# An opening stage of a mixer layer: squares and key weight behind the high parts, low parts on VectorE, projections by halves

## Chip, cores and metric

One NeuronCore of a Trainium2 chip runs the whole program. The metric is device time of one execution in microseconds, as the median of several runs. TensorE (PE) multiplies matrices, VectorE (DVE) and ScalarE (ACT) work elementwise, GpSimd (POOL) does elementwise work and issues some DMAs, SyncE (SP) issues most DMAs. Each engine runs its own instructions in order.

## The reference, cut to what matters

One layer of a diffusion backbone works on 1152 tokens of width 1024: 1024 noisy tokens and 128 prompt tokens. The opening is the modulated norm and the first projections:

```
def trunk_layer(x, mod, ...):
    shift1, scale1, gate1, shift2, scale2, gate2 = jnp.split(mod, 6, axis=-1)
    h = rmsnorm(x, norm1) * (1 + scale1) + shift1
    mix, new_gla, new_hgrn = hybrid_mixer(h, ...)
    ...
def hybrid_mixer(h, ...):
    q_a, k_a, v_a, g_a, lr_a, q_b, f_b, i_b, g_b = jnp.split(h @ w_in, offsets, axis=-1)
    ...
```

`mod` is `silu(c) @ w_ada + b_ada`. After the projections come two groups of gated linear scans (forward and backward), an output projection, and a convolutional feed-forward layer.

## The kernel before

**Precision.** A product of two float32 matrices is made of three faster ones: each operand is split into a high part (the value rounded to the format `fp32r`) and a low part (the rest), and the kernel adds high x high, high x low and low x high. ScalarE copies the high part (line 133 for a weight, line 505 for the activations `h1h`), and `split_lo` (line 69) subtracts it to leave the low part (`wl`, `h1l`) on VectorE or GpSimd.

**Tiles.** Tokens come in nine tiles of 128, `xt`, and three tiles make a group of 384 (`g`). The groups are worked in the order 2, 1, 0; the text calls them first, second and last. The width of 1024 is eight slices `kt` of 128.

**Opening, step by step.** The modulation is computed by matmuls at line 421 in two halves; `ada_first(i)` turns half `i` into scale and shift columns. `norm_x` normalises one token tile: `rstd_of` sums its squares on ScalarE (line 391, with a read of the accumulator), VectorE makes the mean (`st`, line 392), GpSimd the power -1/2 (line 393), and VectorE scales the tile (line 398). `modulate` then, for each slice `kt`: three transposes on TensorE (line 491) into one of four PSUM buffers, a multiply-add to `tt` on VectorE (line 500) or, for some slices, ScalarE (line 496), the high part on ScalarE (line 505) and the low part (line 69). For the first group, the low parts of the first four slices are on VectorE; all others take GpSimd for even slices and VectorE for odd ones. Low-rank columns are multiplied in two parts of four matmuls (line 550) and copied out (`lrs`, line 577).

**Projections.** `proj_d` (line 519) multiplies one weight of 128 columns with one group: 24 matmuls, for each slice high x high, high x low and low x high. `evac` (line 528) copies the sum out on ScalarE (`qj`, `kj`). `wq` and `wk` are the first two weights of the queue `seq`; every weight's low part in the opening is on GpSimd. The first group's key projection is emitted after the second group's `modulate`, and so on down.

**What sets the order.** Code order gives priorities, and a list scheduler with a timeline of its own places each instruction on its engine; `tc.issue_after(x)` forbids placing an instruction ahead of `x`. `prefetch_w` starts the load of the next weights and their split; while `slots["hold"]` is set, the split is put aside in `slots["held"]` and emitted later by whoever takes it out. Weights have two raw buffers (`raw`) and three of high and of low parts.

After the opening, the value projections (line 639) and the scan of the first groups run together: `o` at line 868 makes the gate logits, `fb`, `Q`, `k`, `m` and `S` are the scan's factors, keys and scores, and `lv` (line 964) its level products on TensorE.

## Time and profile before

| | us |
|---|---|
| median of 3 runs | 1519.8 (1519.39 to 1520.59) |
| the profiled execution, its own time | 1521.21 |
| its span in the profile | 1519.4 |
| TensorE busy in the span | 1465.9 (96%) |
| VectorE busy | 1148.0 (76%) |
| ScalarE busy | 780.5 (51%) |
| GpSimd busy | 709.1 (47%) |

A row of the profile in order of time gives the start, the duration, the engine, the line, the operation, what it writes and reads with its shape, and a count if several are merged; in brackets stands the idle time of the engine before it and what ended it. A row that merges several (x4) spans from the first start to the last end. A row that begins with a name and three numbers divided by slashes gives the shortest, middle and longest duration in ns. The chain in order of time gives start, length, engine and line.

### The profile page before, as it was taken

The numbers are of one execution on the slowest core, as the hardware profiler recorded it, in microseconds if no ns is written. First come the engines' busy times: TensorE is split into PE (matmuls) and PEld (weight loads), VectorE is DVE, ScalarE is ACT, GpSimd is POOL, SyncE is SP. The second block draws the span as 40 slices with busy tenths as digits, with TensorE's granted clock in tenths as the row PEclk, the third lists the DMA queues.
The fourth block names the chain that finished last, engine by engine and source line by source line (L and its number), as shares of the span: only waits on it lengthen the run. The fifth ranks groups of instructions, "written<-read, shape, count | busy, mean of one in ns | idle before, by whom it ended". The sixth has DMA issues, their size and how long they took to land.

```text
span 1519.4 us, 31109 instructions
## 1 busy us (share of the span) xinstructions
PE 1465.9 (96%) x12494; PEld 1246.8 (82%) x12494; DVE 1148.0 (76%) x1731; ACT 780.5 (51%) x1517; POOL 709.1 (47%) x538
## 2 busy tenths in 40 slices
PE   6999999999999999999989999999999999999997
PEld 2799989999898998777777888888888877888886
DVE  3666566664565767755699999999999999689475
ACT  3575667555454555613764454444444444466444
POOL 1602123234233241222238999999999995100001
PEclk9999999999999999999999999999999999999999
DMA  9311111335435464867642655544644567979762
GB/s 341 132 44 48 47 54 52 118 96 190 141 106 183 121 197 128 322 243 245 227 140 76 196 174 123 141 123 135 196 120 137 168 167 228 352 255 371 238 190 115
DMA packets 173802, 253.79 MB, mean 167 GB/s; under 512 B 11828, under 2 KB 113698, under 8 KB 171738
## 3 DMA queue, kind: packets, MB, share of 16 engines
q1 hardware_dynamic: 150455, 173.52, 35.6%
q0 software_dynamic: 22592, 77.60, 16.5%
q8 instruction: 98, 1.61, 0.4%
q10 hardware_dynamic: 611, 0.68, 0.1%
q14 instruction: 46, 0.38, 0.1%
HBM read 191.93 MB, written 82.90 MB: 181 GB/s over the span
## 4 chain that ended last, share of the span: by engine, by line
PE 81%; DMA 5%; DVE 5%; issue 3%; ACT 3%; POOL 2%; SPq 0%; POOLq 0%; ACTq 0%; DVEq 0%
PE u L1774 25%; PE mm L625 15%; PE xb L2246 8%; PE yb L2246 6%; PE mm L639 5%; PE x L2005 4%; PE mm L777 3%; PE lv L964 3%; PE yb L2298 2%; PE u L1544 2%; DVE acc L1939 2%; PE x L1032 2%; PE mm L519 1%; DMA raw<-in_w_in_dram 1%; PE ada L1201 1%
## 5 line engine op out<-in xcount | busy, mean ns | idle before, releaser
L1939 DVE SCALAR_TENSOR_TENSOR acc<-u,convc,acc 128x945 f32<-128x945 f32 (+2 forms) x352 | 426.7, 1217 | 7.3 <-ACT acc L1927 0.2
L69 POOL TENSOR_TENSOR wl<-raw,wh 128x1024 fp32r<-128x1024 f32 x42 | 103.3, 2473 | 248.5 <-ACT wh L133 193.4
L625 PE MATMUL mm<-h1h,wh 128*128 128x384 f32 x528 | 185.0, 350 | 0.8 <-ACT qj L528 0.8
L625 PE MATMUL mm<-h1l,wh 128*128 128x384 f32 x528 | 179.0, 339 | 0.0
L625 PE MATMUL mm<-h1h,wl 128*128 128x384 f32 x528 | 179.0, 339 | 0.0
L927 DVE TENSOR_TENSOR Q<-Q,fb 128x384 f32<-128x384 f32 x126 | 81.0, 643 | 82.2 <-PE lv L964 81.3
L69 POOL TENSOR_TENSOR wul<-sr,wuh 128x512 fp32r<-128x512 f32 (+1 forms) x64 | 123.9, 1935 | 14.4 <-ACT wuh L1759 14.3
L69 POOL TENSOR_TENSOR wul<-ra,wuh 128x1024 fp32r<-128x1024 f32 x44 | 117.6, 2673 | 19.1 <-ACT wuh L1759 19.1
L917 ACT ACTIVATE m<-k 128x384 f32<-128x384 f32 x126 | 70.2, 557 | 82.9 <-DVE k L929 40.8
L2220 POOL TENSOR_TENSOR sq<-sq,mhalf 128x1 f32<-128x1 f32 x9 | 11.1, 1232 | 205.3 <-DVE sq L2217 205.3
L625 PEld LDWEIGHTS mm<-h1h,wh 128*128 128x128 f32 x528 | 99.5, 188 | 5.7 <-issue 3.9
L625 PEld LDWEIGHTS mm<-h1l,wh 128*128 128x128 f32 x528 | 99.5, 188 | 0.6 <-issue 0.2
L625 PEld LDWEIGHTS mm<-h1h,wl 128*128 128x128 f32 x528 | 99.3, 188 | 0.8 <-issue 0.5
L929 DVE TENSOR_TENSOR k<-k,fb 128x384 f32<-128x384 f32 x126 | 76.5, 607 | 12.1 <-ACT m L917 7.3
L639 PE MATMUL mm<-wh,h1h 128*128 128x256 f32 x288 | 83.8, 291 | 1.1 <-ACT v L664 0.9
L639 PE MATMUL mm<-wh,h1l 128*128 128x256 f32 x288 | 80.5, 279 | 0.0
L639 PE MATMUL mm<-wl,h1h 128*128 128x256 f32 x288 | 80.4, 279 | 0.0
L133 ACT ACTIVATE wh<-raw 128x1024 fp32r<-128x1024 f32 x50 | 52.8, 1058 | 40.5 <-PE mm L625 11.2
L2037 POOL TENSOR_TENSOR acc<-acc,acc 128x1152 f32<-128x1152 f32 x22 | 62.3, 2834 | 14.8 <-DVE acc L1939 14.8
L1967 ACT ACTIVATE u2p<-u 128x512 f32<-128x512 f32 x44 | 26.4, 601 | 77.8 <-PE u L1774 77.8
L1759 ACT ACTIVATE wuh<-ra 128x1024 fp32r<-128x1024 f32 x42 | 44.3, 1054 | 34.6 <-issue 18.4
L1759 ACT ACTIVATE wuh<-sr 128x512 fp32r<-128x512 f32 (+1 forms) x62 | 48.0, 775 | 19.3 <-PE x L2005 14.4
(386 smaller groups left out, 4483.5 us busy)
## 6 DMA issues: line engine op xcount, KB each, us to landing
ra<-in_w_ffn_up_dram SPq DMA_DIRECT2D x84, 256.0 KB, 3.4
raw<-in_w_in_dram SPq DMA_DIRECT2D x32, 512.0 KB, 4.6
v<-in_w_ada_dram SPq DMA_DIRECT2D x27, 512.0 KB, 4.7
scr_g<-acc POOLq DMA_DIRECT2D x22, 576.0 KB, 5.5
scr_s<-late POOLq DMA_DIRECT2D x11, 1024.0 KB, 5.6
scr_t<-in_w_ffn_down_dram POOLq DMA_DIRECT2D x16, 704.0 KB, 7.3
wa<-in_w_ada_dram SPq DMA_DIRECT2D x16, 512.0 KB, 5.5
scr_t<-in_w_ffn_down_dram POOLq DMA_DIRECT2D x2, 2816.0 KB, 13.0
```

Of the source, the lines that this page charges most:

```text
L69: return eng.tensor_tensor(out, full, hi.bitcast(F32), op=ALU.subtract)
L625: anchor["fill"] = mm(ps, a[:, kt, :], h[kt][b], start=(n == 0), stop=(n == 23))
L639: anchor["fill"] = mm(ps, h[kt][t // 3][:, ts_], a[:, kt % 4, :], start=(n == 0), stop=(n == 23))
L917: nc.scalar.activation(aps(t, 0, [[2 * h, NB], [h, 2], [1, h]]), aps(src, 0, [[2 * h, NB], [BL + h, 2], [1, h]]), AF.Copy)
L927: nc.vector.tensor_tensor(qm, qm, aps(ff_, 2 * h - 1, [[BL - h, 2], [2 * h, NB], [0, h]]), op=ALU.mult)
L929: nc.vector.tensor_tensor(km, km, aps(ff_, BL + 2 * h - 1, [[-(BL + h), 2], [2 * h, NB], [0, h]]), op=ALU.mult)
L1759: first = nc.scalar.activation(hi, raw, AF.Copy)
L1774: last = mm(dst, w_slot(c, a, x)[:, kt, :], HB[y][b][:, kt, :], start=(start and n == 0), stop=(stop and n == 11), skip_group_check=True,)
L1939: last = nc.vector.scalar_tensor_tensor(o, u3[:, r0 + dy : r1 + dy, c0 + dx : c1 + dx], wc(3 * (dy + 1) + dx + 1), o, op0=ALU.mult, op1=AL ...
L2005: last = mm(pk, HB[h]["p"][:, 4 * half + kt, :], aps(flat(W[x]), a * 512 + kt * P, [[(b - a) * 512, 2], [1, P]]), start=(half + kt + n == ...
L2037: last = nc.gpsimd.tensor_tensor(accg, accg, accu, op=ALU.mult)
L2246: anchor["down"] = mm(banks[i], w[a][:, ts_], w[b][:, 512:1024], start=(start and j == 0 and n == 0), stop=(j == NPAIR - 1 and n == 2), sk ...
```

## The change

Six edits, all in the opening:

- The key weight's split is held back at its prefetch (`hold`) and emitted after the first group's `modulate`, to be placed after the first group's last high part (`anchor["first"] = anchor["hi"]`).
- The sums of squares of the other two groups are placed after the key weight's high part (`anchor["first"] = anchor["split"]`).
- The key weight's low part is on VectorE.
- All eight low parts of the first group are on VectorE.
- `proj_d` takes the slices in two halves of four, and in each half all high x high, then all high x low, then all low x high.
- The key projection of each group directly follows its query projection.

```
@@ -130,7 +130,7 @@
         else:
             anchor["load"] = nc.sync.dma_start(raw, srcs)
         def split():
-            nc.scalar.activation(hi, raw, AF.Copy)
+            anchor["split"] = nc.scalar.activation(hi, raw, AF.Copy)
             split_lo(eng, lo, raw, hi)
 
         if slots["hold"]:
@@ -179,8 +179,8 @@
 
 
     seq = []
-    def seq_cols(c):
-        seq.append((1, lambda: w_cols(w_in, c, nc.gpsimd)))
+    def seq_cols(c, eng=nc.gpsimd):
+        seq.append((1, lambda: w_cols(w_in, c, eng)))
 
     def seq_wide(c):
         seq.append((2, lambda: w_wide(w_in, [c], nc.gpsimd)))
@@ -195,7 +195,7 @@
 
     for tau in range(2):
         seq_cols(tau * P)
-        seq_cols(256 + tau * P)
+        seq_cols(256 + tau * P, nc.gpsimd if tau else nc.vector)
         seq_wide(512 + 256 * tau)
     for tau in range(2):
         for i in range(2):
@@ -388,7 +388,8 @@
         if junk is None:
             junk = sq_pool.tile([P, D], BF16, name="junk", tag="junk" + tag, bufs=1)
         st = sq_pool.tile([P, 2], F32, name="st", tag="st" + tag, bufs=4)
-        nc.scalar.activation(junk, x, AF.Square, accum_out=st[:, 0:1])
+        with after("first"):
+            nc.scalar.activation(junk, x, AF.Square, accum_out=st[:, 0:1])
         nc.vector.tensor_scalar(st[:, 0:1], st[:, 0:1], 1.0 / D, EPS, op0=ALU.mult, op1=ALU.add)
         anchor["pow"] = nc.gpsimd.tensor_tensor(st[:, 1:2], st[:, 0:1], mhalf[:, 0:1], op=ALU.pow)
         return st
@@ -440,7 +441,9 @@
     for t in (3, 4, 5, 0, 1, 2):
         load_x(t)
         if t == 5:
+            slots["hold"] = True
             prefetch_w(2)
+            slots["hold"] = False
 
     pt = ps_x.tile([P, 512], F32, name="x", tag="x")
     nc.tensor.transpose(pt[:, 0:P], vrow, ident)
@@ -502,7 +505,7 @@
                 )
             h_, l_ = hi(kt, g), lo(kt, g)
             for (c0, c1, hp_), (_, _, lp_) in zip(h_, l_):
-                nc.scalar.activation(hp_, t[:, c0:c1], AF.Copy)
+                anchor["hi"] = nc.scalar.activation(hp_, t[:, c0:c1], AF.Copy)
                 split_lo(lo_eng[kt % len(lo_eng)], lp_, t[:, c0:c1], hp_)
             if each is not None:
                 each(kt, t)
@@ -514,10 +517,11 @@
         hi, lo = w
         ps = ps_mm.tile([P, BL], F32, name="mm", tag="mm")
         n = 0
-        for kt in range(KT):
+        for kts in (range(4), range(4, KT)):
             for a, h in ((hi, h1h), (hi, h1l), (lo, h1h)):
-                mm(ps, a[:, kt, :], h[kt][b], start=(n == 0), stop=(n == 23))
-                n += 1
+                for kt in kts:
+                    mm(ps, a[:, kt, :], h[kt][b], start=(n == 0), stop=(n == 23))
+                    n += 1
         return ps
 
     def new_pj(nm):
@@ -568,7 +572,7 @@
                 lambda k, g: [(0, BL, h1l[k][g])],
                 ((ps_o, "o"), (ps_lv, "lv")),
                 tp,
-                (nc.vector,) if g == 2 and i == 0 else (nc.gpsimd, nc.vector),
+                (nc.vector,) if g == 2 else (nc.gpsimd, nc.vector),
                 lr_part,
                 (1, 3, 5) if g == 2 else (2, 5),
                 range(4 * i, 4 * i + 4),
@@ -577,16 +581,16 @@
         nc.scalar.activation(lrs, plr, AF.Copy)
         nc.scalar.dma_start(scr_lr[g], lrs)
         if g == 2:
+            anchor["first"] = anchor["hi"]
+            with after("first"):
+                slots["held"].pop(0)()
+            anchor["first"] = anchor["split"]
             wq = next_w()
             first_q[2] = evac(proj_d(wq, 2), "qj", 0.125)
             wk = next_w()
-        elif g == 1:
-            first_k[2] = evac(proj_d(wk, 2), "kj")
-            first_q[1] = evac(proj_d(wq, 1), "qj", 0.125)
         else:
-            first_k[1] = evac(proj_d(wk, 1), "kj")
-            first_q[0] = evac(proj_d(wq, 0), "qj", 0.125)
-            first_k[0] = evac(proj_d(wk, 0), "kj")
+            first_q[g] = evac(proj_d(wq, g), "qj", 0.125)
+        first_k[g] = evac(proj_d(wk, g), "kj")
     mraw = wap_.tile([P, 7, P], F32, name="mraw", tag="wa")
     nc.sync.dma_start(mraw, ins["masks"])
     nc.vector.tensor_copy(masks, mraw)
```

On ScalarE in the first group's second half, the order before was as follows (`h1h4` to `h1h7` are high parts of the first group, `junk` the squares of a token tile, `wh_326` the key weight's high part, `lrs` the low-rank copy):

```order
L391 ACTIVATE junk_544,st_545<-xt_319 128x1024
L505 ACTIVATE h1h4_378<-tt_466 128x384
L133 ACTIVATE wh_326<-raw_325 128x1024
L505 ACTIVATE h1h5_381<-tt_475 128x384
L577 ACTIVATE lrs_502<-mm_412 128x384
L391 ACTIVATE junk_550,st_551<-xt_321 128x1024
L505 ACTIVATE h1h6_384<-tt_484 128x384
L578 DMA scr_lr2_116<-lrs_502 128x384
L391 ACTIVATE junk_556,st_557<-xt_323 128x1024
L505 ACTIVATE h1h7_387<-tt_493 128x384
```

Now on ScalarE, from the same place:

```order
L508 ACTIVATE h1h4_376<-tt_464 128x384
L508 ACTIVATE h1h5_379<-tt_473 128x384
L508 ACTIVATE h1h6_382<-tt_482 128x384
L508 ACTIVATE h1h7_385<-tt_491 128x384
L133 ACTIVATE wh_326<-raw_325 128x1024
L392 ACTIVATE junk_571,st_572<-xt_319 128x1024
L581 ACTIVATE lrs_500<-mm_410 128x384
L392 ACTIVATE junk_577,st_578<-xt_321 128x1024
L582 DMA scr_lr2_116<-lrs_500 128x384
L532 ACTIVATE qj_530<-mm_505 128x384
L392 ACTIVATE junk_583,st_584<-xt_323 128x1024
```

The four high parts moved ahead of the squares and the key weight, and the copy of the query projection now stands ahead of the third square.

On VectorE at the passage from the first group to the second, the order before (`st` is a tile's mean of squares, `xt` its scaling, `masks` the cast of a constant, `tt` a multiply-add of the second group):

```order
L69 TENSOR_TENSOR h1l7_411<-tt_493,h1h7_387 128x384
L392 TENSOR_SCALAR st_693<-st_693 128x1
L398 TENSOR_SCALAR xt_323<-xt_323,st_557 128x1024
L398 TENSOR_SCALAR xt_331<-xt_331,st_693 128x1024
L392 TENSOR_SCALAR st_699<-st_699 128x1
L500 TENSOR_SCALAR tt_567<-x_563,s1_0_340,b1_0_342 128x384
L500 TENSOR_SCALAR tt_575<-x_571,s1_0_340,b1_0_342 128x384
L500 TENSOR_SCALAR tt_591<-x_587,s1_0_340,b1_0_342 128x384
L398 TENSOR_SCALAR xt_333<-xt_333,st_699 128x1024
L592 CAST masks_72<-mraw_867 128x896
```

Now on VectorE, from the scaling of token tile 5 (`xt_323`) on:

```order
L399 TENSOR_SCALAR xt_323<-xt_323,st_584 128x1024
L393 TENSOR_SCALAR st_720<-st_720 128x1
L393 TENSOR_SCALAR st_726<-st_726 128x1
L399 TENSOR_SCALAR xt_329<-xt_329,st_720 128x1024
L596 CAST masks_72<-mraw_867 128x896
L598 CAST low_masks_73<-mraw_867 32x160
L503 TENSOR_SCALAR tt_594<-x_590,s1_0_338,b1_0_340 128x384
L598 CAST low_masks_73<-mraw_867 32x160
L503 TENSOR_SCALAR tt_602<-x_598,s1_0_338,b1_0_340 128x384
L399 TENSOR_SCALAR xt_331<-xt_331,st_726 128x1024
L598 CAST low_masks_73<-mraw_867 32x160
L503 TENSOR_SCALAR tt_618<-x_614,s1_0_338,b1_0_340 128x384
```

The casts, a scaling and two means (tiles 0 and 1) moved ahead of the second group's multiply-adds, which now stand between casts.

On TensorE before the second group's query projection, the order before (`mm_638` is the first group's key projection, `x` a transpose, `mm_562` a low-rank part):

```order
L550 MATMUL mm_562<-tt_575,wlr_311 32x384
L550 MATMUL mm_562<-tt_567,wlr_311 32x384
L491 MATMUL x_623<-ident_74,xt_319 128x128
L491 MATMUL x_623<-ident_74,xt_321 128x128
L491 MATMUL x_623<-ident_74,xt_323 128x128
L519 MATMUL mm_638<-h1h0_366,wh_326 128x384
L519 MATMUL mm_638<-h1l0_390,wh_326 128x384
L519 MATMUL mm_638<-h1h0_366,wl_327 128x384
```

Now on TensorE, from the end of the first group's key projection (`mm_544`) to the second group's first transposes:

```order
L523 MATMUL mm_544<-h1l7_409,wh_326 128x384
L523 MATMUL mm_544<-h1h4_376,wl_327 128x384
L523 MATMUL mm_544<-h1h5_379,wl_327 128x384
L523 MATMUL mm_544<-h1h6_382,wl_327 128x384
L523 MATMUL mm_544<-h1h7_385,wl_327 128x384
L494 MATMUL x_590<-ident_74,xt_319 128x128
L494 MATMUL x_598<-ident_74,xt_319 128x128
L494 MATMUL x_606<-ident_74,xt_319 128x128
```

The whole key projection of the first group moved ahead of the second group's transposes, of which all 24 and a low-rank part now follow it in one piece. The same rows show the halves: the low weights come last.

More of the change, by code (lines that the diff above doesn't have):

```diff
@@ L132, in split @@
         def split():
-            nc.scalar.activation(hi, raw, AF.Copy)
+            anchor["split"] = nc.scalar.activation(hi, raw, AF.Copy)
             split_lo(eng, lo, raw, hi)
@@ L390, in rstd_of @@
         st = sq_pool.tile([P, 2], F32, name="st", tag="st" + tag, bufs=4)
-        nc.scalar.activation(junk, x, AF.Square, accum_out=st[:, 0:1])
+        with after("first"):
+            nc.scalar.activation(junk, x, AF.Square, accum_out=st[:, 0:1])
         nc.vector.tensor_scalar(st[:, 0:1], st[:, 0:1], 1.0 / D, EPS, op0=ALU.mult, op1=ALU.add)
@@ L442 @@
         if t == 5:
+            slots["hold"] = True
             prefetch_w(2)
+            slots["hold"] = False
     pt = ps_x.tile([P, 512], F32, name="x", tag="x")
@@ L516, in proj_d @@
         n = 0
-        for kt in range(KT):
+        for kts in (range(4), range(4, KT)):
             for a, h in ((hi, h1h), (hi, h1l), (lo, h1h)):
-                mm(ps, a[:, kt, :], h[kt][b], start=(n == 0), stop=(n == 23))
-                n += 1
+                for kt in kts:
+                    mm(ps, a[:, kt, :], h[kt][b], start=(n == 0), stop=(n == 23))
+                    n += 1
         return ps
@@ L570 @@
                 tp,
-                (nc.vector,) if g == 2 and i == 0 else (nc.gpsimd, nc.vector),
+                (nc.vector,) if g == 2 else (nc.gpsimd, nc.vector),
                 lr_part,
@@ L579 @@
         if g == 2:
+            anchor["first"] = anchor["hi"]
+            with after("first"):
+                slots["held"].pop(0)()
+            anchor["first"] = anchor["split"]
             wq = next_w()
```

16 lines of the change are left out of this document (6 added, 10 removed).

## The prediction

> **What bounds the kernel now.** I read the page's chain first, then busy time by stage, then TensorE's rows in the opening in order of time, and last ScalarE, VectorE and GpSimd in the same stretch.
>
> ```profile
> PE 81%; DMA 5%; DVE 5%; issue 3%; ACT 3%; POOL 2%; SPq 0%; POOLq 0%; ACTq 0%; DVEq 0%
> ```
>
> ```profile
> 36.00:39.40 3.40, 3.21 (x13) 0.51 1.03 408
> 39.40:47.76 8.36, 4.94 (x30) 1.00 0.86 315
> 47.76:78.07 30.31, 30.27 (x194) 1.00 0.22 63
> ```
>
> The chain is TensorE for 81% of the span. The three windows (stretch, its length, TensorE's busy time, granted clock, DMA share, GB/s) hold the opening: from 47.76 to 78.07 us TensorE does not stop, so a saving before 47.76 carries to the end unless a new wait eats it. Before 47.76 it does stop: 3.4 us idle between 39.40 and 47.76, and ahead of that 3.4 us at half clock.
>
> ```profile
> 35.29 0.45 PE L519 MATMUL mm<-h1h,wh 128*128 128x384 f32 x1 [2.21 <-ACT wh L133]
> 42.44 0.44 PE L519 MATMUL mm<-h1l,wh 128*128 128x384 f32 x1 [0.86 <-DVE h1l L69]
> 44.72 0.65 PE L491 MATMUL x<-ident,xt 128*128 128x128 f32 x4 [1.50 <-DVE xt L398]
> 47.76 1.46 PE L491 MATMUL x<-ident,xt 128*128 128x128 f32 x9 [1.07 <-DVE tt L500]
> 60.72 0.34 PE L519 MATMUL mm<-h1h,wl 128*128 128x384 f32 x1
> ```
>
> The waits are for the query weight's high part, a low part of the first group (`h1l`), a normalised token tile (`xt`) and the next group's multiply-add (`tt`). The last row ends the second group's query projection, at 61.06. The chain in order of time prices TensorE's own pieces:
>
> ```profile
> 50.48 4.17 PE mm L519 x24
> 54.65 0.66 PE x L491 x6
> 67.47 0.78 PE mm L550 x8
> 78.07 5.46 PE mm L639 x48
> ```
>
> A projection of 24 matmuls is 4.17 us (0.174 each), a transpose 0.11, a low-rank part 0.78. At 78.07 the value projections begin; that is the end of the opening.
>
> **The change part by part.** Times below stay on the clock of this profiled execution (span 1519.4, its own time 1521.2). That run lies 1.4 above the median of 1519.8; I subtract the saving from the median.
>
> *First group's projections.* Durations on ScalarE:
>
> ```profile
> 25.43 1.77 ACT L505 ACTIVATE h1h<-tt 128x384 fp32r<-128x384 f32 x4
> 34.18 1.06 ACT L133 ACTIVATE wh<-raw 128x1024 fp32r<-128x1024 f32 x1 [6.98 <-DMA raw<-in_w_in_dram]
> 37.39 1.05 ACT L133 ACTIVATE wh<-raw 128x1024 fp32r<-128x1024 f32 x1
> 42.03 1.05 ACT L391 ACTIVATE junk<-xt 128x1024 bf16<-128x1024 f32 x1
> 43.21 1.06 ACT L391 ACTIVATE junk<-xt 128x1024 bf16<-128x1024 f32 x1
> 46.29 0.49 ACT L528 ACTIVATE qj<-mm 128x384 f32<-128x384 f32 x1 [1.94 <-PE mm L519]
> 63.74 0.66 ACT L496 ACTIVATE tt<-x,b,s 128x384 f32<-128x384 f32 x1
> ```
>
> The query weight lands at 34.18 in both kernels, so TensorE still starts at 35.29. The key weight's split ran at 37.39 without a wait, so its data is there by then. VectorE and GpSimd:
>
> ```profile
> 26.00 1.96 DVE L69 TENSOR_TENSOR h1l<-tt,h1h 128x384 fp32r<-128x384 f32 x4 [0.59 <-ACT h1h L505]
> 33.58 2.41 DVE L500 TENSOR_SCALAR tt<-x,s,b 128x256 f32<-128x256 f32 x6
> 39.64 2.75 DVE L69 TENSOR_TENSOR h1l<-tt,h1h 128x384 fp32r<-128x384 f32 x1
> 44.59 0.55 DVE L69 TENSOR_TENSOR h1l<-tt,h1h 128x384 fp32r<-128x384 f32 x1
> 45.12 0.74 DVE L398 TENSOR_SCALAR xt<-xt,st 128x1024 f32<-128x1024 f32 x1
> 47.03 1.84 DVE L500 TENSOR_SCALAR tt<-x,s,b 128x384 f32<-128x384 f32 x3
> 49.45 0.62 DVE L592 CAST masks<-mraw 128x896 uint8<-128x896 f32 x1
> 50.38 0.63 DVE L594 CAST low_masks<-mraw 32x160 uint8<-32x160 f32 x2
> 54.75 0.92 DVE L398 TENSOR_SCALAR xt<-xt,st 128x1024 f32<-128x1024 f32 x1
> 55.59 3.14 DVE L69 TENSOR_TENSOR h1l<-tt,h1h 128x384 fp32r<-128x384 f32 x3
> ```
>
> ```profile
> 35.32 2.37 POOL L69 TENSOR_TENSOR wl<-raw,wh 128x1024 fp32r<-128x1024 f32 x1 [17.49 <-ACT wh L133]
> 37.65 0.54 POOL L393 TENSOR_TENSOR st<-st,mhalf 128x1 f32<-128x1 f32 x1
> 38.17 1.00 POOL L69 TENSOR_TENSOR h1l<-tt,h1h 128x384 fp32r<-128x384 f32 x1
> 39.13 2.84 POOL L69 TENSOR_TENSOR wl<-raw,wh 128x1024 fp32r<-128x1024 f32 x1
> 51.43 2.40 POOL L69 TENSOR_TENSOR wl<-raw,wh 128x1024 fp32r<-128x1024 f32 x1
> 53.79 4.06 POOL L69 TENSOR_TENSOR h1l<-tt,h1h 128x384 fp32r<-128x384 f32 x3
> ```
>
> The third VectorE row is the heart of it: a subtraction that takes 0.55 alone took 2.75, because GpSimd's subtraction of 39.13 ran until 41.97; it ended 0.42 after that. Subtractions on the two engines run one at a time. With the change the four late high parts run from 36.0 (after the multiply-adds that end at 35.99) to 37.8; VectorE's first low part waits for GpSimd's weight until 37.69, and four at 0.49 end at 39.65, against 45.14 now. That is what the first edit buys. The key weight's high part ends at 38.8, its low part follows the four on VectorE:
>
> ```profile
> L69 DVE TENSOR_TENSOR wl<-raw,wh x8: 1215/1224/2300, 1296.3 to 1491.4; 128x1024 fp32r<-128x1024 f32 x8
> ```
>
> 1.22 at the median, so it ends at 40.9. TensorE's work for the query is 4.17 + 0.78 (the low-rank part): 0.7 of it is done by 36.0, 1.7 during the half-clock stretch (half of 3.4, which the gap before 35.29 causes in both kernels), the other 2.55 by 41.95. The key projection needs nothing later than 40.9 and ends at 46.1. The regrouping by halves adds no matmul; it only lets eight matmuls run ahead of GpSimd's weight, which ends at 37.69. Taken back, it would make the later slices wait for that weight from 36.0 to 37.69: 1.7 us at most, and at half clock.
>
> So at 46.1 query and key are done. Now the key ends at 54.65, but with 15 transposes (1.65) and a low-rank part (0.78) of the next group behind it. Without any new wait the gain would be 54.65 − (46.1 + 2.4) = 6.1 us. That is the ceiling.
>
> *What is late next: the second group.* The moved squares cost nothing by themselves (1.18 from start to start); their place does. In the new order three of them stand behind the query's evacuation: key split to 38.8, square of tile 3 to 40.0, low-rank copy to 40.5, tile 4 to 41.7, evacuation (needs 41.95) to 42.45, tiles 5, 0, 1 to 43.6, 44.8, 46.0, key evacuation to 46.65, tile 2 to 47.85, one multiply-add to 48.5, the value weight's high part to 49.5. VectorE is ready with tile 5 at 45.3 (square 43.6, power 0.54, scale 0.74, and their links), in time for 46.1, but the order then puts the two statistics of tiles 0 and 1 next, and the second waits for 46.0. Behind that wait are queued: scale of tile 0 (to 46.9), the masks (47.4) and one small mask (47.7), and only then the first multiply-add: 48.3, where now the first of the three at 47.03 starts at 47.03. With small masks and the scale of tile 1 between them, the multiply-adds of slices 0, 1, 3, 4 and 6 end at 48.3, 49.2, 50.85, 51.8 and 52.4. TensorE, which has four transpose buffers, stops meanwhile.
>
> GpSimd can start the value weight's low part at 49.95, when the scale of tile 1 lets go, and ends at 52.3. From there both engines have one queue: four low parts at 1.00 on GpSimd, one power at 0.54, four at 0.45 on VectorE (0.55 less the overlap), the scale of tile 2 at 0.5: 6.84 us. Before, the same kind of queue (three at 1.00, four at 0.45, one scale at 0.5: 5.3) ran from 53.83 to 58.73, 4.9 us, so 7% less than its sum. The last low part thus comes between 58.65 and 59.15; I take 58.9, halfway. Behind it the query projection has five matmuls and the array's drain, 1.0: it ends at 59.9 instead of 61.06. **Saving: 1.1 us of the ceiling of 6.1.**
>
> [...]
>
> *The rest.* From 61.06 to 78.07 TensorE needs 17.0 us, all of it work. The new order has the same pieces, but the last group's 12 late transposes now stand behind the key projection: at 59.9 + 4.17 + 0.78 + 1.32 = 66.2 the last query starts, and reaches its last low part 20 matmuls later, at 69.7. ScalarE and VectorE need about the same: last multiply-add 67.2, high part 68.1, and one subtraction each on GpSimd and VectorE, 69.7. No slack: 0 to 0.5 us, and I take 0. No DMA is moved in the opening; the value weight's second buffer is freed at 40.9 instead of 41.97.
>
> *The scan after it.* The change also reorders the first groups' scan. Two multiplies of the second chain now stand ahead of the first chain's first product on VectorE.
>
> ```profile
> DVE Q L927 <- PE lv L964: 30.0, 15, 5.2
> ```
>
> ```profile
> 100.00:120.00 20.00, 19.42 (x467) 18.18 (x465) 15.02 (x34) 11.53 (x33) 6.39 (x4) 1.00 0.14 36
> ```
>
> VectorE waits for TensorE's level products there, 30.0 us between 78 and 230, and TensorE is busy for 19.42 of 20 us: projections cover the scan. I price the reordering at 0, between 0.5 of gain (the idle time in that window) and the price of rival B.
>
> Sum: 1519.8 − 1.1 = 1518.7 us.
>
> **The rivals.** *A, the opening fills.* If the engines' subtractions overlapped after all, VectorE's own work would set the end: from 46.15 the scales of tiles 0, 1 and 2 (2.2), masks 0.55, four small masks 1.2, six multiply-adds at 0.6, four low parts at 0.49: 9.5 us, 55.65, the query ends at 56.65, 4.4 us earlier: 1515.4. For it: scales and masks may hide in GpSimd's gaps. Against it: the row at 39.64, and 3.14 for three low parts in the row at 55.59. These leave it 0.2. [...]
>
> *B, the scan starts late.* The first product on VectorE waits for a multiply of the second chain (0.57, half of a pair of 1.14), a second one stands ahead of the key's first level, and each waits for ScalarE's activation before it: 1.3 to 2.5 us for the first level. It decides if TensorE reaches the first level's products before they are ready, that is, if more than the 15 extra value matmuls placed ahead of them (1.7 us at 5.46 for 48) are needed. Each later level then arrives late too. At 2.5 a wait of up to 0.8 is left at the first level; if three or four levels repeat it, 2.5 to 3 us are lost: 1518.7 + 2.8 = 1521.5. For it: the chain of the first group is dependent from level to level. Against it: VectorE waits for TensorE there, not the other way. 0.12.
>
> *C, nothing arrives.* A later wait that does not move with the opening takes the 1.1 back: 1519.8. For it: DMA is 5% of the chain. Against it: those transfers are released by the work that moves. 0.08.
>
> **How the numbers follow.** The forecast has 0.6, with its own range from 1517.2 (the queue at 58.65, both neutral terms at their gain, a key projection half a microsecond earlier) to 1520.3 (query and key a microsecond later through ScalarE's evacuation, 0.5 in the last group). A measurement of this kernel can tell about 0.2%, 3.0 us, from no change. Faster by more: most of A (0.19) and a tail of the forecast (0.06), 0.25. Slower by more: under half of B (0.05) and what I cannot see in the reordered scan (0.06), 0.11. The rest, 0.64, is within. The range reaches to A's 1515.4 with a little beyond, and past B's 1521.5: 1515.0 to 1521.9.
>
> **What would show it.** Right: the first group's last low part near 39.7, key projection done near 46, TensorE idle between 47.5 and 51 waiting for `tt` and then for `h1l` or `xt`, the second query ending near 60, value projections starting near 77. Step by step: if the key ends later than 47, the half clock or ScalarE's evacuations were mis-sized; if the second group's last low part comes before 57, A; if TensorE idles for level products between 78 and 140, B. It would be wrong altogether if the value projections started before 74.5 or after 79.

## Result, and the profile after

| | median, us | range | runs | ratio to the kernel before |
|---|---|---|---|---|
| before, first series | 1520.19 | 1519.39 to 1521.21 | 4 | |
| after, first series | 1529.24 | 1526.85 to 1530.57 | 4 | 1.0054, interval [1.0042, 1.0066] |
| after, once more (e8_again) | 1524.54 | 1521.51 to 1529.46 | 7 | 1.0029 [1.0016, 1.0042] |

The change made the kernel slower by 0.3 to 0.5%, where 1.1 us of gain and "within 0.2%" were forecast; both series lie outside the range of 1515.0 to 1521.9 by their medians. Executions of one kernel lie further apart than the first numbers showed: 95 of the kernel before, taken beside the experiments, run from 1516.63 to 1524.78 with a median of 1520.6.

The opening did in the profiled execution what was forecast (other executions did not; see "Where the opening's gain went"). These rows of the changed kernel, in order of time, are the first group's late low parts and the key weight's low part on VectorE, the key's copy, the first multiply-add, the second group's last low part, the second query's copy, the last group's low parts and the last key's copy:

```profile
37.03 3.03 DVE L69 TENSOR_TENSOR h1l<-tt,h1h 128x384 fp32r<-128x384 f32 x4 [0.95 <-ACT h1h L508]
39.99 1.21 DVE L69 TENSOR_TENSOR wl<-raw,wh 128x1024 fp32r<-128x1024 f32 x1
46.71 0.49 ACT L532 ACTIVATE kj<-mm 128x384 f32<-128x384 f32 x1 [0.22 <-PE mm L523]
48.07 0.66 DVE L503 TENSOR_SCALAR tt<-x,s,b 128x384 f32<-128x384 f32 x1
58.51 0.55 DVE L69 TENSOR_TENSOR h1l<-tt,h1h 128x384 fp32r<-128x384 f32 x1
60.38 0.49 ACT L532 ACTIVATE qj<-mm 128x384 f32<-128x384 f32 x1
67.72 2.37 DVE L69 TENSOR_TENSOR h1l<-tt,h1h 128x384 fp32r<-128x384 f32 x2
76.37 0.47 ACT L532 ACTIVATE kj<-mm 128x384 f32<-128x384 f32 x1
```

and the last of them in the kernel before:

```profile
77.60 0.47 ACT L528 ACTIVATE kj<-mm 128x384 f32<-128x384 f32 x1
```

| step | forecast | after |
|---|---|---|
| first group's last low part ends | 39.65 | 40.06 |
| key weight's low part ends | 40.9 | 41.20 |
| first multiply-add of the second group ends | 48.3 | 48.73 |
| second group's last low part ends | 58.9 | 59.06 |
| last group's last low part ends | 69.7 | 70.09 |
| last key copied, ahead of the kernel before | 1.1 | 1.23 |

The loss lies behind it. If the two traces' TensorE rows are paired by their number from the end, the changed kernel is 1.5 us ahead at 78 us, 2.8 behind at 250, 0.5 behind at 677, 2.2 to 2.7 behind from 804 to 1265, and 5.7 behind from 1293 to the end. (Most of what comes back by 677 is clock: the kernel before ran 6.8 us at half clock near 633, the changed one 3.4. The queues' order differs there too, from 631 to 637, but no loss shows: 2.7 behind at 620, 1.1 at 640. The 1.6 us from 792 to 804 are the last section's.) Two places carry most of the loss. The first is TensorE at 100 to 120 us, by windows and by its row (the kernel before waited 0.35 at this point):

```profile
100.00:120.00 20.00, 17.10 (x477) 16.09 (x476) 13.45 (x30) 10.79 (x28) 4.67 (x2) 0.91 0.06 10
```

```profile
110.12 0.24 PE L968 MATMUL lv<-Q,m 64*32 64x32 f32 x2 [2.68 <-DVE S L986]
```

```profile
108.76 0.24 PE L964 MATMUL lv<-Q,m 64*32 64x32 f32 x2 [0.35 <-DVE S L982]
```

The second is far from every edit, where the up-projections end and the first down-projection (`xb`) begins. The kernel before waits there once for VectorE (`u`) and once for GpSimd's low part of a weight (`wul`); the changed one waits twice, both times for `wul`. First before, then after:

```profile
1266.89 0.50 PE L1774 MATMUL u<-t4h,wuh 128*128 128x512 f32 x1 [0.89 <-DVE u L2137]
1272.86 0.50 PE L2246 MATMUL xb<-wul,wuh 128*128 128x512 f32 x1 [1.13 <-POOL wul L69]
```

```profile
1275.10 0.50 PE L2250 MATMUL xb<-wul,wuh 128*128 128x512 f32 x1 [1.86 <-POOL wul L69]
1283.98 0.50 PE L2250 MATMUL xb<-wul,wuh 128*128 128x512 f32 x1 [1.78 <-POOL wul L69]
```

GpSimd's rows say why. Before, then after:

```profile
1265.79 1.01 POOL L2038 DMA_DIRECT2D scr_g<-acc  x1
1266.40 1.73 POOL L1894 TENSOR_TENSOR late<-acc 128x512 f32<-128x512 f32 x1
1267.66 2.82 POOL L69 TENSOR_TENSOR wul<-ra,wuh 128x1024 fp32r<-128x1024 f32 x1
1270.01 2.80 POOL L69 TENSOR_TENSOR wul<-sr,wuh 128x1024 fp32r<-128x1024 f32 x1
...
1277.06 2.82 POOL L69 TENSOR_TENSOR wul<-sr,wuh 128x1024 fp32r<-128x1024 f32 x1
```

```profile
1265.71 3.26 POOL L69 TENSOR_TENSOR wul<-ra,wuh 128x1024 fp32r<-128x1024 f32 x1 [7.92 <-ACT wuh L133]
...
1272.28 2.76 POOL L69 TENSOR_TENSOR wul<-sr,wuh 128x1024 fp32r<-128x1024 f32 x1
...
1279.32 0.96 POOL L2042 DMA_DIRECT2D scr_g<-acc  x1
1279.96 1.66 POOL L1898 TENSOR_TENSOR late<-acc 128x512 f32<-128x512 f32 x1
1281.21 2.71 POOL L69 TENSOR_TENSOR wul<-sr,wuh 128x1024 fp32r<-128x1024 f32 x1
```

The scheduler, which lays every queue by a timeline of its own, put the first `wul` ahead of everything else here, so that the second, for which TensorE waits at 1273, comes at 1272.28 instead of 1270.01, 2.3 later, where TensorE is 1.5 later; and it moved the store and the subtraction `late` from the front of this stretch to just ahead of the last `wul`, for which TensorE waits at 1282. On the page the chain changes in the same sense: TensorE's share falls from 81% to 78%, GpSimd's doubles.

```profile
PE 78%; DVE 5%; POOL 4%; issue 3%; DMA 3%; ACT 3%; SPq 0%; POOLq 0%; ACTq 0%; DVEq 0%
```

### The profile page after: what moved, and what is told of

It is laid out like the page before. It is cut to its first block, busy times and chain, and to the rows that moved or that the text cites. A ratio compares the mean times of both kernels' runs of the same rounds, so it can differ in the third digit from the quotient of the medians.

```text
span 1525.1 us, 31105 instructions
## 1 busy us (share of the span) xinstructions
PE 1469.9 (96%) x12494; PEld 1250.8 (82%) x12494; DVE 1146.3 (75%) x1734; ACT 781.7 (51%) x1517; POOL 702.3 (46%) x535
## 4 chain that ended last, share of the span: by engine, by line
PE 78%; DVE 5%; POOL 4%; issue 3%; DMA 3%; ACT 3%; SPq 0%; POOLq 0%; ACTq 0%; DVEq 0%
PE u L1778 22%; PE mm L629 16%; PE xb L2250 7%; PE yb L2250 6%; PE mm L643 5%; PE x L2009 3%; PE lv L968 3%; PE mm L781 3%; PE yb L2302 2%; PE u L1548 2%; PE x L1036 1%; PE mm L523 1%; POOL wul L69 1%; DVE acc L1943 1%; PE ada L1205 1%
## 5 line engine op out<-in xcount | busy, mean ns | idle before, releaser
L69 POOL TENSOR_TENSOR wl<-raw,wh 128x1024 fp32r<-128x1024 f32 x41 | 99.8, 2447 | 252.3 <-ACT wh L133 228.7
L931 DVE TENSOR_TENSOR Q<-Q,fb 128x384 f32<-128x384 f32 x126 | 85.7, 680 | 81.6 <-PE lv L968 80.7
L69 POOL TENSOR_TENSOR wul<-sr,wuh 128x512 fp32r<-128x512 f32 (+1 forms) x64 | 119.6, 1869 | 17.4 <-ACT wuh L1763 17.3
L933 DVE TENSOR_TENSOR k<-k,fb 128x384 f32<-128x384 f32 x126 | 72.1, 572 | 12.9 <-ACT m L921 6.6
L1763 ACT ACTIVATE wuh<-ra 128x1024 fp32r<-128x1024 f32 x42 | 44.3, 1054 | 34.9 <-issue 18.7
L643 PEld LDWEIGHTS mm<-wh,h1h 128*128 128x128 f32 x288 | 54.7, 190 | 4.3 <-ACT v L668 1.9
```

Source lines behind the costliest of these rows:

```text
L69: return eng.tensor_tensor(out, full, hi.bitcast(F32), op=ALU.subtract)
L643: anchor["fill"] = mm(ps, h[kt][t // 3][:, ts_], a[:, kt % 4, :], start=(n == 0), stop=(n == 23))
L931: nc.vector.tensor_tensor(qm, qm, aps(ff_, 2 * h - 1, [[BL - h, 2], [2 * h, NB], [0, h]]), op=ALU.mult)
L933: nc.vector.tensor_tensor(km, km, aps(ff_, BL + 2 * h - 1, [[-(BL + h), 2], [2 * h, NB], [0, h]]), op=ALU.mult)
```

## Experiments

Most of the kernels below (those with a row `QUEUES`) put parts of the queues back in the order that they have in the kernel before, and leave every instruction and every wait for data as it is. This is added at the end of the program; the numbers are those of the instructions as traced, a pair in round brackets is a range, and each is only forbidden to be issued ahead of the one before it in its row:

```
+    traced = {i.name: i for i in nc.cur_bb.bb.instructions}
+    nosync = mybir.DependencyInfo(mybir.DependencyClass.NoSync, mybir.DependencyReason.DATA)
+    for row in QUEUES:
+        row = [n for r in row for n in (range(*r) if isinstance(r, tuple) else (r,))]
+        row = [f"I-{n}" for n in row if f"I-{n}" in traced]
+        for p, q in zip(row, row[1:]):
+            tc.add_manual_dep(traced[q], p, nosync, reason="queue")
```

Ratios are to the kernel before in the same series.

| run | opening | scan's order | end's order | median, us (runs) | ratio |
|---|---|---|---|---|---|
| e1_tail | after | after | before | 1525.99 (5) | 1.0034 [1.0022, 1.0046] |
| e2_scan | after | before | after | 1523.95 (10) | 1.0022 [1.0011, 1.0032] |
| e3_both | after | before | before | 1521.11 (12) | 1.0003 [0.9994, 1.0011] |
| e4_before_tail | before | before | after | 1523.16 (12) | 1.0016 [1.0006, 1.0026] |
| e11_before_scan | before | after | before | 1525.48 (5) | 1.0037 [1.0024, 1.0049] |
| e12_dve_alone | one edit | before | after | 1523.78 (12) | 1.0023 [1.0012, 1.0033] |
| e6_gates | after | one row back | after | 1523.40 (8) | 1.0014 [1.0002, 1.0026] |
| e7_first | after | two rows back | after | 1525.23 (10) | 1.0031 [1.0019, 1.0042] |
| e5_value | weight later | before | before | 1519.63 (12) | 0.9996 [0.9986, 1.0005] |
| e9_value | weight later still | before | before | 1520.41 (11) | 0.9995 [0.9986, 1.0005] |
| e10_lean | and masks later | before | before | 1517.89 (11) | 0.9984 [0.9975, 0.9992] |

### The two orders, one by one

**e1_tail**: the changed kernel with these rows for GpSimd, VectorE and SyncE.

```
+QUEUES = [
+    [13765, (13767, 13769), 13925, 13927, 13926, 14064, 14130, 14134, 14142, 14146, 14138, (14060, 14062)],
+    [(13918, 13923), 14004, 13923, 14005, 14186, 14019, 14021],
+    [14188, (14191, 14193), (14223, 14225), (14239, 14241), (14207, 14209), 14244],
+]
```

> The changed kernel, with only the queue order at the end of the up-projections (around 1262 to 1290 us, on GpSimd, VectorE and SyncE) put back to that of the kernel before. Theory Q (queue orders): what is lost comes from two places where the scheduler laid the queues out anew, the first group's scan (78 to 250 us) and this one. Here GpSimd's store of `scr_g` and its `late` subtraction stand ahead of a weight's low part again, so TensorE's two waits for `wul` (1.86 and 1.78 us) shrink to one of about 1.1 and the half-clock stretch behind them goes: 3 to 4.5 us back, 1521.0 to 1523.5 where the kernel before takes 1519.8. Theory W (clock windows): the order is nothing, TensorE's half-clock stretches of 3.4 us fall where its gaps happen to meet a running window; this kernel stays within 1 us of the changed one, 1526 to 1530, with stretches near 793 and 1285 us. Theory L (the opening itself costs later): also 1526 to 1530, without any difference at the end.

**e2_scan**: rows for TensorE, VectorE and ScalarE between 78 and 250 us as before, the end as after.

> The changed kernel, with only the order of the first groups' scan (78 to about 250 us, on TensorE, VectorE and ScalarE) put back to that of the kernel before; the end of the up-projections keeps the changed kernel's order. Theory Q: TensorE's wait of 2.68 us at 107.4 goes back to about 0.35, the half-clock stretch behind it goes too, and the stream of TensorE stands 1.5 us ahead of the kernel before at 250 us instead of 2.8 behind; of these 4.3, some 2 are taken back at 630 to 680 us, where the kernel before waits for something that does not move. The end still costs 3 to 4.5. Sum 1521.5 to 1524.5. Theory W: 1526 to 1530. Theory L: 1526 to 1530, the loss between 78 and 250 stays whatever the order.

**e3_both**: all rows from the value projections on as before.

> The changed kernel's opening, and every queue from the value projections on in the order of the kernel before. Theory Q: what is left is the opening's gain, 1.5 us at 78 us, as far as no later wait takes it: 1518.3 to 1520.0 against 1519.8, and no half-clock stretch near 110, 793 or 1285 us. Theory W: 1524 to 1530, with stretches at other places. Theory L: 1524 to 1527.

**e4_before_tail**: the three rows of e1_tail in the order of after, on the kernel before.

> The kernel before, with nothing of the change but the changed kernel's queue order at the end of the up-projections. Theory Q: the two waits for `wul` and the half-clock stretch appear here too, 1522.8 to 1524.5, that is 3 to 4.5 us over the kernel before. Theory W and theory L: within 1 us of the kernel before, 1519 to 1521.

Theory Q holds. With the end put back (e1_tail) one wait of about one microsecond is left there; put into the kernel before (e4_before_tail), the two waits appear:

```profile
1276.76 0.50 PE L2250 MATMUL xb<-wul,wuh 128*128 128x512 f32 x1 [1.01 <-POOL wul L69]
```

```profile
1271.45 0.50 PE L2246 MATMUL xb<-wul,wuh 128*128 128x512 f32 x1 [1.89 <-POOL wul L69]
1280.36 0.50 PE L2246 MATMUL xb<-wul,wuh 128*128 128x512 f32 x1 [1.82 <-POOL wul L69]
```

With the scan put back (e2_scan) the wait at 110 is 0.36 again, and the sizes come out by the ratios: the end costs 0.16% (e4_before_tail) to 0.19% (e2_scan less e3_both), 2.4 to 2.9 us; the scan 0.31% (e1_tail less e3_both, which also differ in the order near 633), 4.7 us. The traces agree: by the pairing, the scan costs 4.3 us in the first profile, e1_tail and e11_before_scan; the end costs 1.4 in e4_before_tail and 3.0 in e2_scan and the first profile, where a half-clock stretch follows the second wait. e1_tail came out at 1525.99, above my 1521.0 to 1523.5: I had put the end too dear and the scan too cheap; against the second series of the changed kernel (1524.54) e1_tail shows no gain at all, so the price of the end rests on e4_before_tail, e2_scan and the traces. e3_both came out above my 1518.3 to 1520.0. In it nothing is left of the loss, but the opening's gain isn't there either: -1.1 us would be 0.9993, just outside its interval. Theories L and W fall as explanations of the whole: with both orders back the loss is gone, though half-clock stretches stand in e3_both's profile too.

**e11_before_scan**: the scan's rows of after, on the kernel before.

> The kernel before with nothing of the change but the changed kernel's order in the first groups' scan; its opening and its end stay. Theory Q: the first chain starts about 1.4 later (its gate products stand behind twelve value matmuls) and its first product comes 1.4 later still, so TensorE runs dry near 109 us for 2 to 3 us and has a half-clock stretch behind it: 3 to 5 us over the kernel before at 250 us, 1.5 to 2 of it taken back near 635, 1522.5 to 1525.5. Theory O (the order hurts only together with the new opening): within 1 us of the kernel before, 1519.7 to 1521.7.

```profile
111.27 0.24 PE L964 MATMUL lv<-Q,m 64*32 64x32 f32 x2 [2.69 <-DVE S L982]
```

Theory Q again: the old opening with the new scan order loses 0.37%, 5.6 us, with the same wait.

**e12_dve_alone**: the kernel before with one edit of the change.

```
-                (nc.vector,) if g == 2 and i == 0 else (nc.gpsimd, nc.vector),
+                (nc.vector,) if g == 2 else (nc.gpsimd, nc.vector),
```

> The kernel before with one edit of the change alone: the first group's low parts all on VectorE. The scan keeps the order of the kernel before; the end of the up-projections comes out in the changed kernel's order on GpSimd and SyncE, 1200 us behind the edit, with nothing there edited. Theory Q: the end costs 2 to 3 us as in e4_before_tail, with both waits for `wul` near 1272 and 1281; the opening gives back at most 1 (the last two low parts no longer wait for each other across the engines). 1521.5 to 1523.5, beside 1520.6 for the kernel before. Theory M (moves this small do not last to the end): 1519.5 to 1521.

```profile
1276.41 0.50 PE L2246 MATMUL xb<-wul,wuh 128*128 128x512 f32 x1 [1.86 <-POOL wul L69]
1285.32 0.50 PE L2246 MATMUL xb<-wul,wuh 128*128 128x512 f32 x1 [1.81 <-POOL wul L69]
```

Two subtractions sent to another engine near 40 us turn over GpSimd's queue at 1265 us, and the kernel loses 0.23%, 3.5 us. Not all of that is shown to be the end: by the pairing, its profiled execution falls back by 1.4 us there, as e4_before_tail does, and by 2.9 near 790 and 1.6 near 1254, where half-clock stretches follow waits that the kernel before has too (2.74 and 2.64 us in its profile). Theory Q holds, a little over its range; no gain of the opening shows.

### What in the scan's order costs

The chain of the first group starts with two gate products on TensorE (`o`), two sigmoids on ScalarE (`k<-o`), and on VectorE (`fb`) the factors `Q` and `k` of the first level. Before, then after:

```profile
76.62 1.45 PE L868 MATMUL o<-lr,wup 128*128 128x384 f32 x4
```

```profile
77.97 1.05 ACT L870 ACTIVATE k<-o,vcol 128x384 f32<-128x384 f32 x2
```

```profile
83.95 0.96 DVE L905 TENSOR_TENSOR Q<-fb,qj 128x768 f32<-128x768 f32 x1 [0.35 <-ACT fb L883]
84.87 0.56 DVE L929 TENSOR_TENSOR k<-k,fb 128x384 f32<-128x384 f32 x1
85.34 1.14 DVE L881 TENSOR_SCALAR fb<-o,vcol 128x384 f32<-128x384 f32 x2
```

```profile
77.31 1.45 PE L872 MATMUL o<-lr,wup 128*128 128x384 f32 x4
```

```profile
78.16 1.23 ACT L874 ACTIVATE k<-o,vcol 128x384 f32<-128x384 f32 x2 [1.32 <-PE o L872]
```

```profile
84.67 0.62 DVE L885 TENSOR_SCALAR fb<-o,vcol 128x384 f32<-128x384 f32 x1 [0.71 <-ACT k L874]
85.20 0.95 DVE L909 TENSOR_TENSOR Q<-fb,qj 128x768 f32<-128x768 f32 x1
86.07 0.61 DVE L885 TENSOR_SCALAR fb<-o,vcol 128x384 f32<-128x384 f32 x1
86.60 0.55 DVE L933 TENSOR_TENSOR k<-k,fb 128x384 f32<-128x384 f32 x1
```

The opening ends 1.2 us earlier, but the products now stand behind twelve value matmuls, so the sigmoids start 0.2 later than before. One multiply of the second chain then stands ahead of the first chain's `Q` and both ahead of its `k`, which come 1.25 and 1.7 later. TensorE reaches the end of the work between two levels while the chain is late: 2.68 us of waiting at 107.4. (e11_before_scan has the same wait with the old opening, so TensorE's lead from the new one is not needed for it.)

**e6_gates**: the gate products ahead of the value matmuls.

```
+QUEUES = [[927, 1014]]
```

> The changed kernel and one order more: on TensorE the two gate products of the first chain (`o`, the line of `lr` and `wup`) stand ahead of the first twelve value matmuls again, as in the kernel before. The scheduler orders the rest. Theory S (the chain starts late): the first group's scan is one chain of dependent steps; the twelve matmuls (1.4 us) hold its start at 78.2 although the opening ended 1.5 earlier, and the second chain's two multiplies cost it another 1.4. With the products ahead, the chain starts near 76.6, the wait of 2.68 at 107.4 falls to under 1.0 and no half-clock stretch follows: 3 to 4 us back, 1524.5 to 1526 with the changed kernel's end left as it is. Theory V (the multiplies on VectorE alone): the chain's start is hidden, the wait stays above 2 us, 1527.5 to 1529.5.

**e7_first**: on ScalarE and VectorE the second chain behind the first chain's first level.

```
+QUEUES = [[939, 947, 1308], [1003, 1315]]
```

> The changed kernel and two orders more: on VectorE the second chain's two multiplies stand behind the first chain's key product, on ScalarE its two sigmoids behind the first chain's copy for the level, as in the kernel before. The gate products stay behind the twelve value matmuls. Theory S: the first level comes 1.4 us earlier, the start does not; the wait at 107.4 falls from 2.68 to about 1.3 and brings no half-clock stretch: 2.5 to 3.5 us back, 1525 to 1527. Theory V: all of it comes back, the wait is under 0.5, 1524 to 1525.5.

In e6_gates the long wait is gone altogether (0.22 is the longest of these rows), and the time is 1523.40, below what theory S said. It isn't the products alone: given this one row, the scheduler put the second chain's multiplies back as well. In e7_first the wait is this:

```profile
111.21 0.24 PE L968 MATMUL lv<-Q,m 64*32 64x32 f32 x2 [1.79 <-DVE S L986]
```

Smaller by 0.9, not by 1.4, and still with a half-clock stretch. Its time, 1525.23, lies in the ranges of both theories and can't be told from e8_again's; the wait speaks against theory V. So the late start looks like the larger part, but how much falls to each of the two moves stays open.

### Where the opening's gain went

**e8_again**: the changed kernel unaltered.

> The changed kernel once more, to see whether the places of its loss stay. Theory Q (queue orders): the waits at 107 us (2.7), and of 1.8 twice near 1273 and 1282, are there again, and the time is 1527 to 1530. The half-clock stretches behind the gaps near 790 and 1250, which both kernels have, may come or go, 1.7 us each. Theory R: the opening is either that of the first profile (value projections 1.5 us ahead of the kernel before) or that of e3_both (0.7 behind).

The waits came back: 2.68 at 110.2, 1.87 before 1277.7 and 1.78 before 1286.6. The time did not: 1524.54 lies below theory Q's range. Nor did the opening's gain. VectorE's scale of tile 1 (the second of these rows) and GpSimd's subtraction for the value weight, in the first profile of the changed kernel and in e3_both, whose opening is the same:

```profile
49.69 0.74 DVE L399 TENSOR_SCALAR xt<-xt,st 128x1024 f32<-128x1024 f32 x1
```

```profile
49.83 2.83 POOL L69 TENSOR_TENSOR wl<-raw,wh 128x1024 fp32r<-128x1024 f32 x1 [1.87 <-ACT wh L133]
```

```profile
48.33 2.68 DVE L399 TENSOR_SCALAR xt<-xt,st 128x1024 f32<-128x1024 f32 x1
```

```profile
48.10 2.36 POOL L69 TENSOR_TENSOR wl<-raw,wh 128x1024 fp32r<-128x1024 f32 x1 [2.04 <-ACT wh L133]
```

The scale came 0.14 ahead of GpSimd in the one and 0.23 behind it in the other, and then took 2.68 instead of 0.74, with three multiply-adds queued behind it. TensorE waits 1.66 at 50.4 and runs two windows at half clock:

```profile
50.10:53.50 3.40, 1.74 (x11) 0.20 (x8) 3.29 (x7) 0.88 (x3) 3.23 (x4) 0.50 0.53 127
53.50:56.90 3.40, 3.40 (x16) 3.18 (x13) 3.40 (x6) 1.57 (x4) 3.04 (x2) 0.50 0.12 32
```

Seven profiles have this opening. From the query weight's high part (34.73 in the first) to the last key's copy, the kernel before needs 43.4 us in each of three profiles. The changed opening needs 41.6 and 41.9 where the scale came first (after, e1_tail), and 43.9 to 45.5 where GpSimd came first (the other five). In four of these five the query weight landed before the modulation was ready for it; counted from the later of the two, the five need 43.4 to 44.3, and all seven 43.2 in the mean, 0.2 less than the kernel before.

In the two good ones TensorE had run at half clock for 3.4 us between 35 and 40; in the five others it had not. Counted from the first group's last high part, the first key's copy starts 8.5 and 8.7 us later in the two, 7.3 to 7.6 in the five; ScalarE's value weight stands behind it, and GpSimd's subtraction starts 11.6 and 11.9 later against 10.4 to 10.9. So in these seven profiles the gain came only where a stretch at half clock had held GpSimd back. That fits e3_both, which shows no gain. What each took went with the order of the two starts. Where the scale came first (by 0.14 in after, 0.15 in e1_tail), it took 0.74, and GpSimd's subtraction 2.83 and 2.82. Where GpSimd came first (by 0.23 to 0.96), its subtraction took 2.35 or 2.36, and the scale 1.94 to 2.68, ending 0.54 or 0.55 after it.

**e5_value**: e3_both, and on GpSimd the value weight's low part (537) behind the second group's low parts. Of this run and the next two only the rows for the opening are shown; the others hold the rest in the order of the kernel before.

```
+    [729, 597, 613, 735, 633, 649, 537, 745],
```

> The changed kernel's opening with every queue from the value projections on in the order of the kernel before, as in the run e3_both, and one thing more: on GpSimd the value weight's first low part stands behind the second group's low parts instead of ahead of them. Theory R (a race in the opening): with the change this weight's subtraction and VectorE's scale of tile 1 become ready within a microsecond of each other; where the scale comes first (the changed kernel's profile, 49.69 against 49.83) the opening gains 1.5 us, where GpSimd comes first (e3_both, 48.10 against 48.33) the scale takes 2.7 instead of 0.75, four multiply-adds queue behind it, TensorE runs two windows at half clock, and the opening loses 0.7. Taken out of the way, the scale takes 0.75, the second group's last low part comes 1.5 to 2.5 us earlier, near 57, the value projections start 3 to 4 us ahead of the kernel before, and the time is 1516.5 to 1518.5, beside about 1520.5 for the kernel before. Theory N (nothing of the opening arrives, because a later wait does not move): 1519.5 to 1521.5.

Theory R missed its number. The scale took 0.74, as it said, but the projections ended 0.9 ahead of the kernel before, not 3 to 4, and the time is as before. The weight found another victim, VectorE's last low part of the second group; beside GpSimd's subtraction for the weight (55.80, for 2.81) the last two took 3.19, which take 1.02 in e9_value:

```profile
56.31 3.19 DVE L69 TENSOR_TENSOR h1l<-tt,h1h 128x384 fp32r<-128x384 f32 x2
```

**e9_value**: the same part moved on, to where VectorE waits for TensorE.

```
+    [729, 597, 613, 735, 633, 649, 745, 761, 537, 781],
```

> As e5_value, but the value weight's first low part stands on GpSimd behind the last group's second low part (near 63 us), where VectorE waits for TensorE, instead of directly behind the second group's low parts, where in e5_value it held VectorE's last one from 57 to 59.5. Theory R: the scale of tile 1 takes 0.75 whichever weight lands first, the second group's last low part ends near 57.5, the value projections start about 2 us ahead of the kernel before in every profile, no two windows at half clock near 51, and the time is 1517.5 to 1519.5, where the kernel before takes 1520.7. Theory N: 1519.7 to 1521.5.

**e10_lean**: with two moves more; VectorE's mask casts (869 to 873) behind the second group's low parts, ScalarE's square of tile 2 (733) and the value weight's high part (536) behind first high parts. GpSimd's row also has a low part (633) and a power (735) the other way round.

```
+    [729, 597, 613, 633, 735, 649, 745, 761, 537, 781],
+    [588, 722, 728, 724, 595, 603, 619, 730, 631, 647, 605, 621, 655, 734, 641, 736, 657, (869, 874), 743],
+    [570, 611, 596, 733, 604, 536, 639],
```

> As e9_value, with two moves more in the opening: VectorE's five mask casts stand behind the second group's low parts instead of ahead of and between its multiply-adds, and ScalarE's square of tile 2 and the value weight's high part behind the first high parts of the second group. Theory R: TensorE's two waits of 0.87 and 0.81 near 48 and 50 shrink to under 0.5 each, the value projections start about 3 us ahead, 1516.5 to 1518.5. Theory N: 1519.7 to 1521.5.

e9_value can't be told from the kernel before and lies in theory N's range; in its profile the scale of tile 1 took 1.52, beside a low part on GpSimd (48.59, for 1.01), and one half-clock stretch stands at 51.0. In e10_lean TensorE's waits in the second group shrink to one:

```profile
48.87 1.20 PE L494 MATMUL x<-ident,xt 128*128 128x128 f32 x9 [0.65 <-ACT tt L499]
```

```profile
75.18 0.47 ACT L532 ACTIVATE kj<-mm 128x384 f32<-128x384 f32 x1
```

The last key is copied at 75.18, 2.4 ahead of the kernel before, and 1517.89 is 0.16% below it [0.9975, 0.9992]. It is faster than both kernels, and lies in what theory R said for it.

## Why the prediction was wrong

- *First group's projections, second and last group*: right in the profiled execution, each step within 0.5 us, the saving 1.23 against 1.1 (the prediction's own terms, 61.06 − 59.9, give 1.16). That agreement was partly luck. The half-clock stretch that the prediction counted on "in both kernels" came in two of the seven profiles of the changed opening. And "GpSimd can start the value weight's low part at 49.95, when the scale of tile 1 lets go" took for granted who comes first. The margin was 0.14 us, and in five of seven profiles the other engine was first. What is left of the 1.1 over many executions is nothing that twelve of them show (e3_both, 1.0003). What GpSimd's subtraction costs VectorE was priced for the low parts (2.75 instead of 0.55 in the kernel before) and not for this scale (2.68 instead of 0.74 in e3_both).
- *"I price the reordering at 0"* is the step that failed most. It costs 4.7 us (e1_tail less e3_both) to 5.6 (e11_before_scan). The reason given, that VectorE waits for TensorE there and projections cover the scan, read the rows the wrong way round: the same window had TensorE idle for 0.58 us before the change, 0.35 of it waiting for this chain, so at that point the chain had no slack, and its delay went straight into TensorE's wait, 2.68 instead of 0.35.
- *Rival B* had the mechanism, and its sign (TensorE idle for level products between 78 and 140) is what the trace shows: the second chain's multiplies and the first product behind them, 1.3 to 2.5 us late, measured 1.25 and 1.7. It was given 0.12 and too small a price: it left out the gate products behind twelve value matmuls, put the wait at the first level instead of at 107 us, and left out the half-clock stretch behind it.
- *The end at 1265 to 1290 us* was in no part of the sum. The prediction compared orders in the opening and in the first scan; the queues were also laid anew a thousand microseconds later, at 2.4 to 2.9 us (e4_before_tail; e2_scan less e3_both).
- *Rivals A and C*: A is excluded by the last low part at 59.06. C's "a later wait that does not move" is not what took the gain: in e10_lean an earlier opening does arrive.
- *3.0 us as what a measurement can tell* was too small for a few executions: two series of the same changed kernel gave 1529.24 and 1524.54.

The sum by the runs: opening a loss of 0.03%, scan 0.31%, end 0.16 to 0.19%, together about 0.5%, 7.6 to 8.1 us. The first series gave 0.54%, the second 0.29%, whose interval ends at 0.42%: the sum is a little above what that series allows, and the size of the whole loss is known no better than 0.3 to 0.5%. The direction and the two places are shown; the size is not.

The ends of the forecast's own range do not add up exactly either: their terms give about 1516.95 and 1520.2, not 1517.2 and 1520.3. Nothing hangs on it.

## What to carry to other kernels

Where a scheduler lays the queues, compare its order over the whole program, and price first every place where the bottleneck engine already waits a little, since nothing covered a delay there in this kernel: 0.35 us of waiting became 2.68. A gain that rests on one engine coming a tenth of a microsecond ahead of another is a coin toss, here won by 0.14 and 0.15 us in two profiles of seven: move the long operation out of the way. And test an opening with the rest of the program held in its old order, or what is measured is the scheduler.

## What was not expected of the hardware

In these profiles TensorE's half-clock stretches begin on a grid: within a profile their starts lie whole multiples of 3.413 us apart (in the first profile of the changed kernel from 14.81 to 793.05, 228 of them; in that of the kernel before from 15.43 to 629.83, 180), and the grid lies otherwise in each execution. One step of the grid is called a cell here. What followed a wait went with the idle time within one cell. Both kernels wait 2.74 us near 789. Before, the grid cut that wait in two and the clock stayed; after, 2.40 of it fell in one cell and the next ran at half clock:

```profile
786.84:790.26 3.42, 1.88 (x10) 1.25 (x8) 3.42 (x3) 3.42 (x5) 3.11 (x1) 1.00 0.00 0
790.26:793.67 3.41, 2.22 (x10) 1.84 (x11) 3.38 (x3) 0.74 (x2) 3.41 (x3) 1.00 0.26 77
```

```profile
789.64:793.05 3.41, 1.01 (x4) 0.86 (x5) 3.41 (x2) 1.95 (x4) 3.41 (x2) 1.00 0.22 64
793.05:796.46 3.41, 3.41 (x9) 2.65 (x8) 3.37 (x6) 0.11 (x1) 3.41 (x2) 0.50 0.04 13
```

Over the 14 profiles, from 20 to 1500 us, cells at full clock with more than 2.0 us idle were followed by half clock 28 times of 28; with 1.7 to 2.0 idle 18 of 24; with 1.5 to 1.7, 3 of 18; with 0.9 to 1.5, 2 of 135; with 0.5 to 0.9, none of 192. So in these profiles half of a cell idle, 1.7 of 3.41 us, was mostly enough, and a wait near 1.8 us had two prices. The two waits near 1273 and 1282 set TensorE back by 1.4 us against the kernel before in e4_before_tail, and by 3.0 in e2_scan, where a half-clock stretch follows the second. That is also a part of the spread of executions: over the 95 of the kernel before, the time falls as the granted clock rises, with a correlation of -0.50, which is a quarter of the variance.
